# Weights' sums, key products and the gate-to-key transform change engines in the first stage of a hybrid encoder block

## The chip, the core and the metric

The kernel runs on one core of a Trainium2 chip. Its time is the device time of one execution in microseconds (us); of several executions the median is taken. TensorE (PE, with its weight load PEld) does the matmuls, VectorE (DVE), ScalarE (ACT) and GpSimd (POOL) the elementwise work, and SyncE (SP) issues most DMAs. Each engine works through its own instructions in order.

## The reference

One encoder block on 1024 tokens of width 1024, all float32. What matters here is one combined projection and what follows from it:

```
h = layer_norm(x)
p = h @ W_in        # 11776 columns: q/k/v of 3 head groups, HGRN q, f_fwd, f_bwd, i, g, 2 merge gates
a = dilated_attention(q, k, v)                       # 4 pairs of heads, three dilations
f = lb + (1 - lb) * sigmoid(f_pre);  k = 1 - f       # per direction; the gate gives the key
q_dec, k_inv = q * exp(cumsum(log f)), k * exp(-cumsum(log f))   # in chunks of 64 tokens
o = intra-chunk scores + state recurrence, forward and backward, 8 heads of 128
m = sigmoid(g_a) * (a @ W_a) + sigmoid(g_r) * (r @ W_r)
h = layer_norm(alpha * h + m @ W_o);  h = layer_norm(alpha * h + SwiGLU(h))
```

## The kernel before

The large products are done as Strassen-Winograd products of halves: seven products instead of eight for each 2x2 of blocks. Every operand is split into a high part (rounded to the fast float32 format) and the rest, and each product is three matmuls a 128-row block (`mm3`, L301 hi*hi, L302 hi weight * lo activation, L303 lo weight * hi activation).

The **first stage** (`phase1`, to about 1160 us of the span) makes the combined projection. `stream` runs over 23 sets of four 128-column tiles; in a set two groups `g` of two tiles each go through the products in the order 1, 2, 6, 5, 7, 3, 4. A product is 12 matmuls of 512 columns. Its weights are one of the four loaded blocks a11, a12, a21, a22 (128 partitions x 512, named `wa` in the profile) or one of the sums s1 = a21 + a22 (`ws`, L574), s3 = a11 - a21 (the **third sum**, L575, written over a21), s2 = s1 - a11 (L576, written over a11, so it comes after L575 has read a11) and s4 = a12 - s2 (L579). s2 is wanted by product 6, s3 only by product 7. For each product ScalarE casts the weights to `w_hi` (L585) and VectorE subtracts to `w_lo` (L590); four buffers of each exist, and the two are recorded three products ahead. Results leave PSUM by `keep` (ACT, L606) and by adds on VectorE (L475, L486, L507, L513).

Beside the stream runs the **side work**, a unit at a time: HGRN of a head, and the attention of a pair of heads. It fills the engines between the stream's instructions. `hgrn_dir` is run for each head and direction, 16 times. ScalarE makes four gate arrays from the loaded tanh (`t0` or `t1`, 128x1024; L1272, names fa, fb, qd, finv). Then the same tile is turned in place from gate to key, t3 = gna*t3 + ga (L1286). VectorE scans fa and fb into decays (L1291), t3's near half is multiplied by the decays R of fb (L1300), VectorE scans G (in qd), t3's far half is multiplied by G (L1303), VectorE scans finv, and two products with q (L1306, L1307) end it. Tiny copies of decays (`dec`, `both`, L1311 to L1314), memory sets and some small scalar work are GpSimd's. The key tile is then transposed on PE (L1322).

The order of each engine's instructions is set by a scheduler that models the engines at build time: the stream's casts, sums and evacuations have a priority 1000 instructions ahead, ScalarE's side work is kept behind the stream's latest (`behind`), and the first 14 products (`opening`) keep the order in which they are written.

Of the kernel before, what the change touches and what calls it, by code (L numbers as in the profile page):

```python
# [13 lines left out]
AF = mybir.ActivationFunctionType  # L14
OP = mybir.AluOpType
# [66 lines left out]
class Group:  # L82
# [25 lines left out]
    def product(self, n, bank, first):  # L108
        o = self.o
        if n not in self.made:  # L110
            self.prep(n)
        hi, lo = self.made.pop(n)
        xhi, xlo = o.xb[o.PRODUCTS[n][1]]
        if first:
            self.banks[bank] = o.ps_pj() if (bank == 2) != self.swap else o.ps_sd()
        ps = self.banks[bank]
        for k in range(4):
            o.mm3(ps, hi[:, k, :], lo[:, k, :], xhi[:, k, :], xlo[:, k, :], first and k == 0, k == 3,
                  skip_group_check=True)
        return ps  # L120
# [29 lines left out]
class Block:  # L150
# [405 lines left out]
    def stream(self, tiles):  # L556

        nc, tc = self.nc, self.tc
        self.cols = [c for c, _ in tiles]
        seq = [(n, g, p) for n in range(len(tiles) // 4) for p in self.ORDER for g in range(2)]  # L560
        after = {6: "a11", 7: "a21", 3: "a12", 4: "a22"}
        A = [{}, {}]
        state = [[{}, {}], [{}, {}]]
        ready = {}

        def sums(i, third=nc.gpsimd):
            if i >= len(seq):
                return
            n, g, p = seq[i]
            a = A[g]  # L570
            with tc.high_priority(offset=self.evac_ahead):
                if p == 6:
                    a["s1"] = self.blk.tile([128, 4, 128], F32, name="ws1", tag=f"s1{g}", bufs=1)
                    nc.vector.tensor_add(a["s1"], a["a21"], a["a22"])  # L574
                    third.tensor_sub(a["a21"], a["a11"], a["a21"])  # L575
                    nc.vector.tensor_sub(a["a11"], a["s1"], a["a11"])  # L576
                    a["s3"], a["s2"] = a["a21"], a["a11"]
                elif p == 3:
                    nc.vector.tensor_sub(a["a12"], a["a12"], a["s2"])  # L579
                    a["s4"] = a["a12"]  # L580

        def cast(i):
            n, g, p = seq[i]
            ready[i] = self.granules()
            nc.scalar.copy(ready[i][0], A[g][self.PRODUCTS[p][0]])  # L585

        def rest(i, e):
            n, g, p = seq[i]
            hi, lo = ready[i]
            e.tensor_sub(lo, A[g][self.PRODUCTS[p][0]], hi.bitcast(F32))  # L590
            if p in after and 4 * n + 4 < len(tiles):
                A[g][after[p]] = self.block(n + 1, g, after[p])

        def prep(i):
            if i >= len(seq):
                return
            with tc.high_priority(offset=self.evac_ahead):
                cast(i)
                rest(i, nc.vector)

        def bank(n, g, b):
            return self.ps_pj(2 * g + (n + b) % 2)

        def keep(ps, tag):
            t = self.ws.tile([128, HALF], F32, name="wkeep", tag=tag, bufs=1)
            nc.scalar.copy(t, ps)  # L606
            return t

        def product(i, h=None):
            n, g, p = seq[i]  # L610
            s = state[n % 2][g]
            if p in (1, 2) and h != 1:
                s[p] = bank(n, g, p)
            ps = s[1 if p in (1, 6, 7, 4) else 2]
            hi, lo = ready[i]
            if h != 0:
                del ready[i]
            c = slice(0, HALF) if h is None else slice(256 * h, 256 * h + 256)
            xhi, xlo = self.xb[self.PRODUCTS[p][1]]
            for k in range(4):  # L620
                self.mm3(ps[:, c], hi[:, k, :], lo[:, k, :], xhi[:, k, c], xlo[:, k, c],
                         p in (1, 2, 5) and k == 0 and h != 1, k == 3,
                         skip_group_check=True)

        def evacuate(i, *later):
            n, g, p = seq[i]
            s = state[n % 2][g]
            ps = s[1 if p in (1, 6, 7, 4) else 2]
            pair = [f for _, f in tiles[4 * n + 2 * g:4 * n + 2 * g + 2]]
            with tc.high_priority(offset=self.evac_ahead):  # L630
                if p in (1, 6):
                    s["u"] = keep(ps, f"k1{g}")
                elif p == 5:
                    s["m5"] = keep(ps, f"k5{g}")
                elif p == 2:
                    pair[0](0, ps, s["u"], *later)
                elif p == 7:
                    pair[1](1, ps, s["m5"])
                elif p == 3:
                    pair[0](1, ps, s["u"])  # L640
                else:
                    pair[1](0, ps, None)

        self.ahead_of = {}
        first = 2 * len(self.ORDER)
        with self.pool("p0") as pool:
            self.lasts = {}
            with self.in_order():
                self.opening(pool, A, {(g, p): i for i, (_, g, p) in enumerate(seq[:first])}, first, cast, rest, sums,
                             product, evacuate)  # L650
        yield 4
        sums(first + 4)
        for i, (n, g, p) in enumerate(seq):
            if i < first:
                continue
            with self.noted():
                sums(i + 5)
                prep(i + 3)
            if i < first + 2:
                continue  # L660
            product(i)
            evacuate(i)
            yield 4 * n + 2 * g + 2 if p == 4 else 0

    def opening(self, pool, A, at, first, cast, rest, sums, product, evacuate):

        nc, R = self.nc, self.rows_in(pool)
        dve, gps = nc.vector, nc.gpsimd
# [99 lines left out]
        R.sum("t1", 5)  # L768
        R.hi("t1", 5)
        R.copy(5, 1, "act")  # L770
        sums(at[0, 6], dve)
        R.turn(7, 0, 1)
        R.lo("t1", 5)
        cast(at[0, 6])
# [6 lines left out]
        R.sum("t1", 6)  # L781
        R.hi("t1", 6)
        product(at[0, 6], 0)
        sums(at[1, 6], dve)
        cast(at[1, 6])
        evacuate(at[0, 2], later)
        cast(at[0, 5])
# [464 lines left out]
    def hgrn_dir(self, h, d, st):  # L1252

        nc = self.nc
        ga, gb, gna = (z[:, d, h:h + 1] for z in (self.ga, self.gb, self.gna))
        t3 = st[f"t{d}"].rearrange("p (c i) -> p c i", i=128)
# [3 lines left out]
        far = slice(64, 128) if fwd else slice(0, 64)  # L1260
        near = slice(0, 64) if fwd else slice(64, 128)
# [3 lines left out]
        G = qd[:, 0:4, :].rearrange("p a (b i) -> p (a b) i", i=64)  # L1265
        H = self.half("finv").rearrange("p (c i) -> p c i", i=64)
        ends = self.half("ends").rearrange("p (c i) -> p c i", i=64)
        R = B[:, :, 1:65]

        def gates(f, one, to, of):  # L1270
            nc.gpsimd.memset(f[:, :, one:one + 1], 0.0)
            nc.scalar.activation(f[:, :, to], t3[:, :, of], AF.Identity, bias=gb, scale=ga)  # L1272
# [8 lines left out]
        else:  # L1281
# [1 line left out]
            gates(B, 0, slice(1, 66), slice(63, 128))  # L1283
            gates(G, 0, hi, slice(0, 63))
            gates(H, 63, lo, slice(64, 127))
        nc.gpsimd.tensor_scalar(t3, t3, gna, ga, op0=OP.mult, op1=OP.add)  # L1286

        def scan(f, at, rev):
            f = f.rearrange("p c i -> p (c i)")
            f = f[:, ::-1] if rev else f  # L1290
            nc.vector.tensor_tensor_scan(f, f, at, 0.0, op0=OP.mult, op1=OP.add)  # L1291

        def inverse(f, of, rev):

            nc.vector.reciprocal(ends[:, :, 0], of[:, ::-1] if rev else of)
            scan(f, ends.rearrange("p c i -> p (c i)"), rev)

        scan(A, self.d1[64], not fwd)
        scan(B, self.d1[66], fwd)
        nc.gpsimd.tensor_mul(t3[:, :, near], t3[:, :, near], R)  # L1300
        yield
        inverse(G, A[:, :, 63 if fwd else 0], fwd)
        nc.gpsimd.tensor_mul(t3[:, :, far], t3[:, :, far], G)  # L1303
        yield
        inverse(H, R[:, :, 0 if fwd else 63], not fwd)
        nc.vector.scalar_tensor_tensor(qd[:, :, far], q3[:, :, far], CQ, A, op0=OP.mult, op1=OP.mult)  # L1306
# [912 lines left out]
```

## Time and profile before

| | us |
|---|---|
| median of 3 runs | 2072.26 (2071.73 to 2073.45) |
| the profiled execution's own time | 2073.43 |
| its span | 2071.7 |
| busy: PE / DVE / ACT / POOL | 2013.5 / 1407.2 / 975.6 / 792.0 |

Busy time is summed over the whole span, which has stages with different limits; the first stage is about 56% of it. A matmul's span overlaps the next one's, so that 222 matmuls of 512 columns fill 50 us (0.226 us from start to start) though each is shown with about 0.39 us. In views by line, "mean ns" is that of one instruction; in views of a single line, three numbers are minimum, median and maximum. Waits of PE name the instruction that came last.

### The profile page before, as it was taken

The page shows a single profiled execution, that of the slowest core. Times are in us where ns is not written, and L with a number is a line of the kernel's source. Part 1 is how long each engine was busy: PE and PEld are TensorE (multiplying, and loading weights), DVE is VectorE, ACT ScalarE, POOL GpSimd, SP SyncE. Part 2 cuts the span into 40 slices and gives each one's busy share as a digit, 9 for nine tenths or more (in the row PEclk, how much of TensorE's full clock was granted, in tenths as well). Part 3 has the DMA queues.
Part 4 walks back from the last instruction along what each step waited for, and adds up shares of the span by engine and source line. Part 5 has one row for each costly group of instructions (what it writes and reads, how often), then busy time and mean ns, then how long its engine had stood idle before and what let it go on. Part 6 is the DMA issues. An engine that isn't in the chain of part 4 may idle for free.

```text
span 2071.7 us, 31393 instructions
## 1 busy us (share of the span) xinstructions
PE 2013.5 (97%) x11037; PEld 1672.6 (81%) x11037; DVE 1407.2 (68%) x2361; ACT 975.6 (47%) x2039; POOL 792.0 (38%) x694
## 2 busy tenths in 40 slices
PE   5999999999999999999999999999899999999998
PEld 5788888788888888888888788886788888888876
DVE  7778666776477855877556623457777776777864
ACT  7555456554564536655464421244444444444330
POOL 1134310343013330332100263243667767755563
PEclk9999999999999999999999999999999999999999
DMA  5433533445334352444436763335445444458684
GB/s 208 156 122 117 184 114 117 133 131 160 113 123 133 123 166 97 132 149 141 143 96 219 249 228 112 101 119 167 141 143 179 141 169 158 161 169 315 199 266 165
DMA packets 296448, 324.21 MB, mean 156 GB/s; under 512 B 15905, under 2 KB 212834, under 8 KB 296290
## 3 DMA queue, kind: packets, MB, share of 16 engines
q1 hardware_dynamic: 290272, 302.05, 45.2%
q10 hardware_dynamic: 6018, 20.16, 2.4%
q8 instruction: 87, 1.43, 0.3%
q14 instruction: 71, 0.58, 0.1%
HBM read 211.78 MB, written 110.36 MB: 156 GB/s over the span
## 4 chain that ended last, share of the span: by engine, by line
PE 77%; DVE 8%; DMA 5%; issue 4%; ACT 3%; POOL 2%; DVEq 0%; SPq 0%; ACTq 0%; POOLq 0%
PE pj L301 17%; PE pj L303 17%; PE pj L302 16%; PE sd L301 6%; PE sd L303 6%; PE sd L302 6%; PE sd L1391 2%; DVE w_lo L590 2%; DMA wa<-in_w_in_dram 2%; PE sd L1338 1%; POOL w_lo L280 1%; DMA ghi<-gs3h 1%; PE sd L1206 1%; ACT pf L1011 1%; PE sd L1131 1%
## 5 line engine op out<-in xcount | busy, mean ns | idle before, releaser
L590 DVE TENSOR_TENSOR w_lo<-wa,w_hi 128x512 fp32r<-128x512 f32 x273 | 213.8, 787 | 100.3 <-ACT w_hi L585 97.7
L585 ACT CAST w_hi<-wa 128x512 fp32r<-128x512 f32 x276 | 169.7, 618 | 215.4 <-PE pj L302 167.9
L280 POOL TENSOR_TENSOR w_lo<-f_raw,w_hi 128x512 fp32r<-128x512 f32 x110 | 176.0, 1611 | 107.1 <-ACT w_hi L276 45.7
L575 POOL TENSOR_TENSOR wa<-wa,wa 128x512 f32<-128x512 f32 x44 | 67.3, 1531 | 245.0 <-DVE ws L574 156.3
L301 PE MATMUL pj<-xt1hi,w_hi 128*128 128x512 f32 (+1 forms) x276 | 107.3, 389 | 0.0
L301 PE MATMUL pj<-xb22hi,w_hi 128*128 128x512 f32 x268 | 105.6, 394 | 1.6 <-ACT wkeep L606 1.6
L303 PE MATMUL pj<-xt1hi,w_lo 128*128 128x512 f32 (+1 forms) x276 | 106.3, 385 | 0.4 <-POOL w_lo L280 0.4
L302 PE MATMUL pj<-xt1lo,w_hi 128*128 128x512 f32 (+1 forms) x276 | 106.3, 385 | 0.0
L276 ACT CAST w_hi<-f_raw 128x512 fp32r<-128x512 f32 x110 | 67.9, 619 | 80.1 <-DVE f_raw L100 31.7
L302 PE MATMUL pj<-xb22lo,w_hi 128*128 128x512 f32 x268 | 104.8, 391 | 0.0
L303 PE MATMUL pj<-xb22hi,w_lo 128*128 128x512 f32 x268 | 104.7, 391 | 0.0
L280 POOL TENSOR_TENSOR w_lo<-Wb,w_hi 128x512 fp32r<-128x512 f32 x47 | 64.8, 1380 | 58.1 <-ACT w_hi L276 55.2
L606 ACT COPY wkeep<-pj 128x512 f32<-128x512 f32 x138 | 80.1, 581 | 8.6 <-DVE evh L513 3.9
L301 PE MATMUL pj<-xt2hi,w_hi 128*128 128x512 f32 (+1 forms) x196 | 77.9, 397 | 5.1 <-ACT w_hi L585 3.1
L301 PE MATMUL pj<-xb11hi,w_hi 128*128 128x512 f32 (+1 forms) x196 | 76.9, 392 | 3.3 <-ACT w_hi L585 2.5
L303 PE MATMUL pj<-xt2hi,w_lo 128*128 128x512 f32 (+1 forms) x196 | 76.6, 391 | 2.9 <-DVE w_lo L590 2.0
L303 PE MATMUL pj<-xb21hi,w_lo 128*128 128x512 f32 (+1 forms) x196 | 75.9, 387 | 3.4 <-DVE w_lo L590 3.4
L280 POOL TENSOR_TENSOR w_lo<-wsum,w_hi 128x512 fp32r<-128x512 f32 x44 | 66.9, 1520 | 30.2 <-ACT w_hi L276 26.3
L303 PE MATMUL pj<-xb11hi,w_lo 128*128 128x512 f32 (+1 forms) x196 | 76.5, 390 | 1.1 <-POOL w_lo L590 0.6
L302 PE MATMUL pj<-xt2lo,w_hi 128*128 128x512 f32 (+1 forms) x196 | 76.5, 390 | 0.7 <-DVE xt2lo L432 0.7
L301 PE MATMUL pj<-xb21hi,w_hi 128*128 128x512 f32 (+1 forms) x196 | 76.9, 392 | 0.1
L301 PE MATMUL pj<-xt3hi,w_hi 128*128 128x512 f32 x188 | 75.2, 400 | 1.5 <-ACT w_hi L276 1.5
(435 smaller groups left out, 6380.6 us busy)
## 6 DMA issues: line engine op xcount, KB each, us to landing
wa<-in_w_in_dram SPq DMA_DIRECT2D x184, 256.0 KB, 3.1
f_raw<-in_w_ffn_in_dram SPq DMA_DIRECT2D x44, 512.0 KB, 4.3
Wb<-in_w_ffn_out_dram SPq DMA_DIRECT2D x40, 256.0 KB, 5.3
tg<-evh SPq DMA_DIRECT2D x32, 256.0 KB, 2.1
tg<-tg SPq DMA_DIRECT2D x16, 512.0 KB, 4.3
y<-ahs SPq DMA_DIRECT2D x16, 512.0 KB, 4.1
ah<-xt SPq DMA_DIRECT2D x8, 512.0 KB, 6.5
rec<-hg ACTq DMA_DIRECT2D x8, 512.0 KB, 5.3
```

The source lines that it names most:

```text
L276: nc.scalar.copy(hi, src)
L280: e.tensor_sub(lo, src, hi.bitcast(F32))
L301: nc.tensor.matmul(ps, whi, xhi, start=first, stop=False, **kw)
L302: nc.tensor.matmul(ps, whi, xlo, start=False, stop=False, **kw)
L303: nc.tensor.matmul(ps, wlo, xhi, start=False, stop=last, **kw)
L575: third.tensor_sub(a["a21"], a["a11"], a["a21"])
L585: nc.scalar.copy(ready[i][0], A[g][self.PRODUCTS[p][0]])
L590: e.tensor_sub(lo, A[g][self.PRODUCTS[p][0]], hi.bitcast(F32))
L606: nc.scalar.copy(t, ps)
L1011: nc.scalar.activation(v, v, AF.Exp, bias=N12[:, hd, c:c + 1], scale=QSCALE, accum_out=l[:, hd, c:c + 1])
L1131: nc.tensor.matmul(ps[:, tt % 2, :], q[pb, 128 * tt - 64:128 * tt + 64], k[pb, 128 * (tt - 1):128 * (tt + 1)], start=True, stop=True)
L1391: nc.tensor.matmul(po[:, jj, :], l, r, start=(n == 0), stop=(n == len(terms) - 1))
```

## The change

Three things move, all in the first stage. The third sum L575 (128x512) of the stream's sets goes from GpSimd to VectorE: 44 of them; the two of the opening are there already. In `hgrn_dir` the transform L1286 (128x1024, in place) goes from GpSimd to ScalarE as one activation with a scale and a bias a partition (16), and the two products L1300 and L1303 (8 chunks of 64 on 128 partitions, in place) go from GpSimd to VectorE (32). The arithmetic stays as it is. GpSimd keeps the small scalar work, copies of decays and memory sets.

```
-        def sums(i, third=nc.gpsimd):
+        def sums(i):
...
                     nc.vector.tensor_add(a["s1"], a["a21"], a["a22"])
-                    third.tensor_sub(a["a21"], a["a11"], a["a21"])
+                    nc.vector.tensor_sub(a["a21"], a["a11"], a["a21"])
                     nc.vector.tensor_sub(a["a11"], a["s1"], a["a11"])
...
-        sums(at[0, 6], dve)
+        sums(at[0, 6])
...
-        sums(at[1, 6], dve)
+        sums(at[1, 6])
...
-        nc.gpsimd.tensor_scalar(t3, t3, gna, ga, op0=OP.mult, op1=OP.add)
+        nc.scalar.activation(t3, t3, AF.Identity, bias=ga, scale=gna)
...
         scan(B, self.d1[66], fwd)
-        nc.gpsimd.tensor_mul(t3[:, :, near], t3[:, :, near], R)
+        nc.vector.tensor_mul(t3[:, :, near], t3[:, :, near], R)
         yield
         inverse(G, A[:, :, 63 if fwd else 0], fwd)
-        nc.gpsimd.tensor_mul(t3[:, :, far], t3[:, :, far], G)
+        nc.vector.tensor_mul(t3[:, :, far], t3[:, :, far], G)
```

The scheduler orders all engines anew; the places are mostly near the moved instructions. Two of them matter below.

**VectorE, third head, from the `w_lo` of block 3718 to the `w_lo` of block 3871** (a12 of group 0, product 2). Before:

```order
L590 TENSOR_TENSOR w_lo_4063<-wa11_3718,w_hi_4062 128x512
L1291 SCALAR_TENSOR_TENSOR fa_3989<-fa_3989,d164_1153 128x512
L1291 SCALAR_TENSOR_TENSOR fb_4081<-fb_4081,d166_1156 128x528
L1306 SCALAR_TENSOR_TENSOR qd_3991<-q_3940,fa_3989 128x8x64
L1307 SCALAR_TENSOR_TENSOR qd_3991<-q_3940,finv_3992 128x8x64
L1295 RECIPROCAL ends_4084<-fa_3989 128x8
L576 TENSOR_TENSOR wa11_3718<-ws1_4124,wa11_3718 128x512
L513 SCALAR_TENSOR_TENSOR evh_4048<-evh_4048,wkeep_3844 128x512
L590 TENSOR_TENSOR w_lo_4103<-wa12_3871,w_hi_4102 128x512
```

With the change:

```order
L590 TENSOR_TENSOR w_lo_4063<-wa11_3718,w_hi_4062 128x512
L1306 SCALAR_TENSOR_TENSOR qd_3991<-q_3940,fa_3989 128x8x64
L1291 SCALAR_TENSOR_TENSOR fa_3989<-fa_3989,d164_1153 128x512
L576 TENSOR_TENSOR wa11_3651<-ws1_4098,wa11_3651 128x512
L1291 SCALAR_TENSOR_TENSOR fb_4081<-fb_4081,d166_1156 128x528
L575 TENSOR_TENSOR wa21_3851<-wa11_3718,wa21_3851 128x512
L1307 SCALAR_TENSOR_TENSOR qd_3991<-q_3940,finv_3992 128x8x64
L590 TENSOR_TENSOR w_lo_4103<-wa12_3871,w_hi_4102 128x512
```

Between the two L590 one L575 has come in; the reciprocal, the L513 and the L576 of group 1 have gone behind, and the L576 of group 0, which stood ahead, is in between.

**VectorE, fifth head, from the forward scan of finv to the `w_lo` of a22 (6117)**, group 0, product 4. Before:

```order
L1291 SCALAR_TENSOR_TENSOR finv_6535<-finv_6535,ends_6536 128x512
L590 TENSOR_TENSOR w_lo_6604<-wa12_6096,w_hi_6603 128x512
L1291 SCALAR_TENSOR_TENSOR fa_6532<-fa_6532,d164_1153 128x512
L1291 SCALAR_TENSOR_TENSOR fb_6626<-fb_6626,d166_1156 128x528
L1295 RECIPROCAL ends_6629<-fa_6532 128x8
L507 TENSOR_TENSOR wkeep_6569<-wkeep_6569,pj_6331 128x512
L1291 SCALAR_TENSOR_TENSOR qd_6627<-qd_6627,ends_6629 128x512
L1306 SCALAR_TENSOR_TENSOR qd_6534<-q_6487,fa_6532 128x8x64
L1307 SCALAR_TENSOR_TENSOR qd_6534<-q_6487,finv_6535 128x8x64
L1295 RECIPROCAL ends_6629<-fb_6626 128x8
L590 TENSOR_TENSOR w_lo_6644<-wa22_6117,w_hi_6643 128x512
```

With the change:

```order
L1291 SCALAR_TENSOR_TENSOR finv_6535<-finv_6535,ends_6536 128x512
L1300 TENSOR_TENSOR t0_6485<-t0_6485,fb_6533 128x8x64
L1303 TENSOR_TENSOR t0_6485<-t0_6485,qd_6534 128x8x64
L590 TENSOR_TENSOR w_lo_6575<-wa12_6036,w_hi_6574 128x512
L1306 SCALAR_TENSOR_TENSOR qd_6534<-q_6487,fa_6532 128x8x64
L1307 SCALAR_TENSOR_TENSOR qd_6534<-q_6487,finv_6535 128x8x64
L590 TENSOR_TENSOR w_lo_6604<-wa12_6096,w_hi_6603 128x512
L1291 SCALAR_TENSOR_TENSOR fa_6532<-fa_6532,d164_1153 128x512
L1291 SCALAR_TENSOR_TENSOR fb_6626<-fb_6626,d166_1156 128x528
L507 TENSOR_TENSOR wkeep_6569<-wkeep_6569,pj_6331 128x512
L1295 RECIPROCAL ends_6629<-fa_6532 128x8
L590 TENSOR_TENSOR w_lo_6644<-wa22_6117,w_hi_6643 128x512
```

The forward products L1300 and L1303 have come in, the `w_lo` of 6036 has gone behind them, and the scan of the backward G (qd) and the second reciprocal have gone behind the last `w_lo`.

**ScalarE, third head, backward direction**, from the last gate on, with the change:

```order
L1272 ACTIVATE finv_4083<-t1_3942,gb_1146,ga_1145 128x8x63
L585 CAST w_hi_4102<-wa12_3871 128x512
L510 ACTIVATE evh_4048<-wkeep_3844 128x512
L489 ACTIVATE evh_4078<-pj_3632 128x512
L1286 ACTIVATE t1_3942<-t1_3942,ga_1145,gna_1147 128x1024
L585 CAST w_hi_4128<-wa12_3948 128x512
```

The L1286 stands between two of the stream's casts; before, it was not on this engine, and L510 stood ahead of the first cast.

## The prediction

> **What bounds the kernel now.** I read the page first:
>
> ```profile
> span 2071.7 us, 31393 instructions
> PE 2013.5 (97%) x11037; PEld 1672.6 (81%) x11037; DVE 1407.2 (68%) x2361; ACT 975.6 (47%) x2039; POOL 792.0 (38%) x694
> ```
>
> PE sets the time, and only what PE waits for in the first stage can be won: the change touches no matmul. So next come PE's waits from 100 to 1155 us (waiter, releaser, us in total, times, longest):
>
> ```profile
> PE pj L303 <- DVE w_lo L590: 6.8, 3, 3.4
> PE sd L1368 <- DVE hR L1352: 1.4, 1, 1.4
> ```
>
> All end with VectorE, most of them with a late `w_lo`. Where they are and what they cost is shown by the engines' busy time in stretches of 2.5 us (PE, PEld, DVE, ACT, POOL, then granted clock, DMA share, GB/s):
>
> ```profile
> 377.50:380.00 2.50, 2.24 (x19) 1.80 (x17) 2.50 (x5) 0.00 (x0) 2.50 (x2) 1.00 0.00 0
> 380.00:382.50 2.50, 0.00 (x0) 0.00 (x0) 2.50 (x3) 1.51 (x3) 2.50 (x4) 1.00 0.06 22
> 382.50:385.00 2.50, 1.87 (x5) 1.48 (x6) 2.50 (x4) 1.62 (x4) 1.34 (x3) 0.67 0.50 188
> 385.00:387.50 2.50, 2.50 (x9) 1.99 (x8) 2.50 (x4) 0.43 (x1) 0.94 (x1) 0.64 0.00 0
> ...
> 627.50:630.00 2.50, 1.88 (x15) 1.45 (x13) 2.50 (x2) 0.00 (x0) 2.42 (x3) 1.00 0.00 0
> 630.00:632.50 2.50, 0.26 (x1) 0.26 (x2) 2.50 (x4) 0.00 (x0) 1.63 (x1) 1.00 0.00 0
> 632.50:635.00 2.50, 2.50 (x7) 1.95 (x7) 2.50 (x4) 1.59 (x3) 0.00 (x0) 0.51 0.59 165
> 635.00:637.50 2.50, 2.50 (x10) 1.99 (x10) 2.50 (x6) 0.64 (x3) 0.00 (x0) 0.81 0.91 320
> ...
> 1157.50:1160.00 2.50, 1.20 (x6) 0.66 (x4) 2.50 (x4) 2.50 (x6) 0.00 (x0) 1.00 0.21 62
> ```
>
> Two stalls stand out, in the third and the fifth head. PE is idle 0.26 + 2.50 + 0.63 = 3.39 us in the first and 0.62 + 2.24 = 2.86 us in the second, and after each the granted clock is down: (0.33 + 0.36) x 2.5 = 1.7 us and (0.49 + 0.19) x 2.5 = 1.7 us of full-speed work lost. Together 9.65 us. In both VectorE is busy without a break and GpSimd beside it. A third place, at the stage's end, loses 1.3 us.
>
> Now VectorE's timeline ahead of the first stall (start, us, instruction), and GpSimd's:
>
> ```profile
> 366.00 1.25 DVE L1291 TENSOR_TENSOR_SCAN fb<-fb,d 128x528 f32<-128x528 f32 x1
> ...
> 373.68 1.14 DVE L590 TENSOR_TENSOR w_lo<-wa,w_hi 128x512 fp32r<-128x512 f32 x1
> 374.74 1.22 DVE L1291 TENSOR_TENSOR_SCAN fa<-fa,d 128x512 f32<-128x512 f32 x1
> 375.88 2.29 DVE L1291 TENSOR_TENSOR_SCAN fb<-fb,d 128x528 f32<-128x528 f32 x1
> 378.09 0.66 DVE L1306 SCALAR_TENSOR_TENSOR qd<-q,fa 128x512 f32<-128x512 f32 x1
> 378.67 0.68 DVE L1307 SCALAR_TENSOR_TENSOR qd<-q,finv 128x512 f32<-128x512 f32 x1
> 379.27 0.19 DVE L1295 RECIPROCAL ends<-fa 128x8 f32<-128x8 f32 x1
> 379.39 1.50 DVE L576 TENSOR_TENSOR wa<-ws,wa 128x512 f32<-128x512 f32 x1
> 380.81 0.68 DVE L513 SCALAR_TENSOR_TENSOR evh<-evh,wkeep 128x512 f32<-128x512 f32 x1
> 381.41 1.67 DVE L590 TENSOR_TENSOR w_lo<-wa,w_hi 128x512 fp32r<-128x512 f32 x1
> ```
>
> ```profile
> 374.85 2.21 POOL L575 TENSOR_TENSOR wa<-wa,wa 128x512 f32<-128x512 f32 x1
> 377.00 1.16 POOL L1311 COPY dec<-fa 128x8 f32<-128x8 f32 x1
> 380.90 1.62 POOL L1300 TENSOR_TENSOR t<-t,fb 128x512 f32<-128x512 f32 x1
> ```
>
> The last `w_lo` is the one PE waits for; it ends at 383.08. The same kind of instruction takes 0.68 or 1.7 us, and a scan 1.2 or 2.3 us, here while GpSimd works. All of the stage, by line (minimum, median, maximum in ns):
>
> ```profile
> L590 DVE TENSOR_TENSOR w_lo<-wa,w_hi x273: 620/686/1797, 28.4 to 1177.8; 128x512 fp32r<-128x512 f32 x137
> L486 DVE TENSOR_TENSOR evh<-wkeep,pj x48: 660/680/690, 48.3 to 1182.6; 128x512 f32<-128x512 f32 x48
> ```
>
> L590 has two inputs in SBUF and reaches 1797 ns; L486, of the same size with one input in PSUM, never goes over 690. So the excess looks like GpSimd and VectorE shutting each other out of SBUF, not like a slow instruction. The Trainium skill says so (SBUF — State Buffer, "SBUF: two separate sides"): a VectorE instruction with two SBUF inputs and a GpSimd one that reads SBUF take one shared port pair in turn, each for its whole length. By that rule a collision costs up to a whole GpSimd instruction and the term below is nearly all of its upper bound; the two rows agree, though they do not show which GpSimd instructions shut VectorE out.
>
> **What the change removes.** From GpSimd 44 third sums, 16 transforms and 32 products go. Grouped by line and shape, 60 to 1155 us (count | busy, mean ns | idle before):
>
> ```profile
> L575 POOL TENSOR_TENSOR wa<-wa,wa 128x512 f32<-128x512 f32 x43 | 66.1, 1537 | 245.0 <-DVE ws L574 156.3 <-DMA wa<-in_w_in_dram 17.0 <-ACT pf L1011 14.2
> L1303 POOL TENSOR_TENSOR t<-t,qd 128x512 f32<-128x512 f32 x16 | 30.8, 1925 | 3.0 <-DVE qd L1291 2.9
> L1286 POOL TENSOR_SCALAR t<-t,gna,ga 128x1024 f32<-128x1024 f32 x16 | 30.1, 1884 | 2.6 <-POOL fb L1271 2.6
> L1300 POOL TENSOR_TENSOR t<-t,fb 128x512 f32<-128x512 f32 x16 | 28.3, 1767 | 0.7 <-DVE fb L1291 0.2
> L590 DVE TENSOR_TENSOR w_lo<-wa,w_hi 128x512 fp32r<-128x512 f32 x261 | 205.5, 791 | 98.3 <-ACT w_hi L585 95.7 <-PE sd L974 2.0 <-PE sd L1028 0.3
> L1291 DVE TENSOR_TENSOR_SCAN finv<-finv,ends 128x512 f32<-128x512 f32 x16 | 26.9, 1680 | 0.5
> ```
>
> GpSimd loses 66.1 + 30.8 + 30.1 + 28.3 = 155 us, all its large work of the stage except the attention bias and one small add. If the excess goes with it, VectorE gets back (791 - 686) x 261 = 27.4 us in L590, and with 1.22 us as the undisturbed scan (the row at 374.74) (1.68 - 1.22) x 16 = 7.4 in one of the four scans: 35 us in these two groups, more with the rest. The bounds of that term are nothing and all of it.
>
> **What it adds.** On VectorE 44 + 32 = 76 instructions of 128x512 from SBUF. Their nearest rows are L576 for the sum and L1306 for the products (the same chunks of 64), both undisturbed about 0.68 us, 0.60 from start to start (378.09, 378.67, 379.27): 76 x 0.60 = 46 us. So VectorE's total hardly moves, -35 + 46 = +11 us at most. What counts is the place. In a head's stretch GpSimd's work is dense, and each L1300 or L1303 removed costs VectorE 0.6 us where a collision costs 0.8 to 1.1.
>
> Ahead of the first stall: from the scan at 366.00 to the `w_lo` at 373.68 VectorE took 7.68 us; in the new order it holds two scans (1.25, 1.22), seven instructions of 0.66 to 0.69 and a reciprocal, about 7.4, less 0.08 of overlap for each, 6.6 us. From there the order shown gives 0.69 + 0.66 + 1.22 + 0.69 + 1.25 + 0.69 + 0.68 = 5.9, less 0.6 of overlap, 5.3 us instead of 7.73. The late `w_lo` then ends at 366.0 + 6.6 + 5.3 + 0.7 = 378.6, and PE, which was idle for the last 0.26 us before 380, wanted it at 379.7: the 3.39 us go, with 1 us to spare. The fifth head's stretch runs from one scan of fb to the `w_lo` that PE waits for:
>
> ```profile
> 617.38 1.26 DVE L1291 TENSOR_TENSOR_SCAN fb<-fb,d 128x528 f32<-128x528 f32 x1 [2.61 <-ACT fb L1272]
> ...
> 630.55 1.63 DVE L590 TENSOR_TENSOR w_lo<-wa,w_hi 128x512 fp32r<-128x512 f32 x1
> ```
>
> It ends at 632.2. In the new order that scan, a reciprocal and the eleven rows shown stand ahead of it: four scans 4.9, two reciprocals 0.4, seven of 0.66 to 0.69 together 4.7, so 10.0 less 1.0 of overlap; it ends at 617.4 + 9.0 + 0.7 = 627.1, against a need at 629.4. But the two `w_lo` that follow come with little or no margin, since the products of the backward direction and the next s1, whose blocks must have landed, now stand ahead of them. At the stage's end L576 waits for an L575 of 3.96 us on GpSimd:
>
> ```profile
> L575 POOL TENSOR_TENSOR wa<-wa,wa x44: 1274/1416/3961, 85.3 to 1155.3; 128x512 f32<-128x512 f32 x44
> ```
>
> On VectorE it takes 0.7, so I count 1 of the 1.3 us there as won.
>
> On ScalarE 16 activations of 128x1024 with scale and bias a partition:
>
> ```profile
> L324 ACT ACTIVATE xt<-xt,mv x8: 1237/1242/1252, 8.3 to 38.5; 128x1024 f32<-128x1024 f32 x8
> L585 ACT CAST w_hi<-wa 128x512 fp32r<-128x512 f32 x261 | 160.5, 618 | 203.9 <-PE pj L302 163.2 <-issue 18.5 <-DVE wa L576 9.1
> ```
>
> The first is the same function, shape and operands: 1.24 us, 16 x 1.24 = 20 us. The casts stand idle 203.9 us, 163 of them until PE frees a buffer, so a cast that comes 1.24 us later is covered three products ahead, by about 12 x 0.226 = 2.7 us each. Without that cover it would cost 1.24 us a time. L1300 must now wait for ScalarE, not for GpSimd; in the orders shown L1286 follows the last gates closely, while VectorE has scans ahead of L1300. If it did not, the next `w_lo` would be queued behind it. No DMA is issued elsewhere, and SP's order changes at a few neighbours only.
>
> **The sum.** Two stalls with their clock -9.65, the stage's end -1.0, and for new small stalls behind the two places and in other heads +3.0 (two of the 1.4 us that the waits show as a small one, rounded up): -7.65 us. The profiled execution took 2073.43 us, 1.2 above the median; its stalls are taken as those of a median run, so 2072.26 - 7.65 = 2064.6, say **2064.5 us**.
>
> **The rivals.** (1) *The stalls only move* (0.14). For it: margins of about 1 us, and VectorE no less busy in total. Against it: the two places have 2 to 4 us less ahead of the late `w_lo`. Half of the idle time and one loss of clock would stay: -9.65 / 2 - 1 + 3 = -2.8, or 2069.5; with a little more, 2071.
>
> (2) *ScalarE is late* (0.10): L1286 stands ahead of casts and of L1300. Against it the casts' 163 us of waiting for PE. If half of the 16 find no cover, 8 x 1.24 = 10 us eat the gain: 2074; it decides where PE's waits name L585 in the heads.
>
> (3) *VectorE becomes the bound*, the other side (0.08). In a head it is nearly full:
>
> ```profile
> 850.00:900.00 50.00, 50.00 (x300) 42.52 (x297) 43.04 (x67) 27.95 (x60) 18.52 (x17) 1.00 0.48 157
> ```
>
> If the excess is not GpSimd's large work, or the tiny copies left there (L1311, 1.16 us) keep causing it, each head gets four products and two sums, 6 x 0.60 = 3.6 us, ahead of a `w_lo`: the two stalls grow by 3.6 and two more heads begin to stall at 3.6 + 1.7 of clock: 7.2 + 10.6 = +18, or 2090; half of it, 2081. It decides once the mean of L590 stays over some 0.75 us. The Trainium skill warns that way (Perfetto Trace Analysis, "Optimizing Scalar/DVE Operations"): work should leave a saturated VectorE, though the same section doubts that GpSimd helps.
>
> **How the numbers follow.** The forecast has 0.68; its own range is 2058 (no new stalls, and some of the small ones gone) to 2068.5. With (1) and the near end of (2) the range is 2057.5 to 2072. A measurement of this kernel tells about 0.2%, 4.1 us. Faster: 0.66 of the forecast, 0.03 of (1) and 0.01 of (2), 0.70. The same: 0.02, 0.11 and 0.06, 0.19. Slower: 0.03 of (2) and 0.08 of (3), 0.11.
>
> **What would show it.** Right: L590 with mean near 0.70 us and hardly one over 1 us; the scans all near 1.2; no stretch in the third and fifth heads with the clock under 1.00; PE waits on L590 of 2 to 4 us in the stage; GpSimd's busy time down by about 155 us or more. Wrong: a PE wait on L585 or behind L1300, or an L590 still at 1.7 us beside a small GpSimd copy.

## The result, and the profile after

The changed kernel takes 2057.11 us (median of 4 runs, 2054.89 to 2059.24) beside 2072.86 us of the kernel before (4 runs in the same set). The ratio is 0.9929, with a 95% interval of 0.9917 to 0.9941: 14.7 us faster, about twice the 7.65 that the sum gave.

The page of the changed kernel, which shows the fastest of its runs, 2054.89 us:

```profile
span 2053.1 us, 31298 instructions
PE 2009.0 (98%) x11037; PEld 1671.5 (81%) x11037; DVE 1401.7 (68%) x2437; ACT 995.8 (49%) x2055; POOL 641.3 (31%) x602
```

The span is 18.6 us shorter (4 us of that beyond the 14.7, as the page before shows a run of 2073.43 us, a little slower than its median, and this page the fastest run). VectorE is as busy as before (1401.7 and 1407.2), and only GpSimd has much less to do. The first stage in one stretch (PE, PEld, VectorE, ScalarE, GpSimd, then granted clock, DMA share, GB/s), before:

```profile
100.00:1150.00 1050.00, 1039.08 (x6676) 870.78 (x6675) 734.07 (x1492) 568.25 (x1326) 270.01 (x317) 1.00 0.43 138
```

and after:

```profile
100.00:1150.00 1050.00, 1049.55 (x6740) 881.59 (x6739) 743.19 (x1588) 596.95 (x1358) 127.53 (x229) 1.00 0.44 142
```

PE was idle for 10.92 us of this stretch and is idle for 0.45 now. The view of PE's waits from 100 to 1155 us, which showed five kinds before, has no row left. The places of the two stalls, in stretches of 2.5 us:

```profile
377.50:380.00 2.50, 2.50 (x18) 2.17 (x17) 2.50 (x4) 2.31 (x5) 1.99 (x2) 1.00 0.43 159
380.00:382.50 2.50, 2.40 (x16) 1.79 (x15) 2.50 (x6) 0.40 (x1) 2.42 (x2) 1.00 0.14 51
382.50:385.00 2.50, 2.50 (x12) 2.06 (x11) 2.50 (x5) 1.26 (x4) 0.24 (x1) 1.00 0.28 105
...
627.50:630.00 2.50, 2.50 (x15) 2.15 (x14) 2.50 (x5) 0.75 (x2) 0.00 (x0) 1.00 0.98 347
630.00:632.50 2.50, 2.50 (x22) 2.41 (x21) 2.50 (x5) 2.38 (x6) 0.00 (x0) 1.00 0.31 115
```

VectorE is still busy without a break, PE works through, and the clock stays at 1.00. The subtractions and scans (the first row from the groups by line, 60 to 1155 us; the others give minimum, median and maximum over the whole run):

```profile
L590 DVE TENSOR_TENSOR w_lo<-wa,w_hi 128x512 fp32r<-128x512 f32 x266 | 185.4, 699 | 102.7 <-ACT w_hi L585 99.4 <-PE sd L974 2.0 <-PE sd L1338 0.9
...
L1291 DVE TENSOR_TENSOR_SCAN finv<-finv,ends x16: 1205/1220/1247, 126.6 to 924.4; 128x512 f32<-128x512 f32 x16
L1286 ACT ACTIVATE t<-t,ga,gna x16: 1230/1248/1257, 124.5 to 921.3; 128x1024 f32<-128x1024 f32 x16
L575 DVE TENSOR_TENSOR wa<-wa,wa x46: 653/684/693, 40.3 to 1138.4; 128x512 f32<-128x512 f32 x46
```

The mean of L590 fell from 791 to 699 ns; the scan of finv, which had a mean of 1680, now never goes over 1247. VectorE's timeline in the third head, up to the `w_lo` that came late before, and GpSimd's beside it:

```profile
368.90 1.25 DVE L1291 TENSOR_TENSOR_SCAN fb<-fb,d 128x528 f32<-128x528 f32 x1
...
376.65 1.22 DVE L1291 TENSOR_TENSOR_SCAN fa<-fa,d 128x512 f32<-128x512 f32 x1
377.79 0.67 DVE L576 TENSOR_TENSOR wa<-ws,wa 128x512 f32<-128x512 f32 x1
378.37 1.25 DVE L1291 TENSOR_TENSOR_SCAN fb<-fb,d 128x528 f32<-128x528 f32 x1
379.54 0.67 DVE L575 TENSOR_TENSOR wa<-wa,wa 128x512 f32<-128x512 f32 x1
380.12 0.68 DVE L1307 SCALAR_TENSOR_TENSOR qd<-q,finv 128x512 f32<-128x512 f32 x1
380.72 0.68 DVE L590 TENSOR_TENSOR w_lo<-wa,w_hi 128x512 fp32r<-128x512 f32 x1
```

```profile
377.93 1.68 POOL L1311 COPY dec<-fa 128x8 f32<-128x8 f32 x1 [7.24 <-DVE fa L1291]
379.68 2.38 POOL L1312 COPY dec<-fb 128x8 f32<-128x8 f32 x1
```

Every instruction of VectorE has its undisturbed length. The small copies beside them take 1.68 and 2.38 us, where the shortest of their kind takes 0.19: here GpSimd waits for VectorE, and no wait for these copies shows in the profile.

### The profile page after: what moved, and what is told of

It reads as the page before. It is cut to its first block, busy times and chain, and to the rows that moved or that the text cites. A ratio compares the mean times of both kernels' runs of the same rounds, so it can differ in the third digit from the quotient of the medians.

```text
span 2053.1 us, 31298 instructions
## 1 busy us (share of the span) xinstructions
PE 2009.0 (98%) x11037; PEld 1671.5 (81%) x11037; DVE 1401.7 (68%) x2437; ACT 995.8 (49%) x2055; POOL 641.3 (31%) x602
## 4 chain that ended last, share of the span: by engine, by line
PE 74%; issue 2%; DVE 1%; POOL 1%; DMA 1%; ACT 1%; DVEq 0%; POOLq 0%; ACTq 0%
PE pj L301 16%; PE pj L303 16%; PE pj L302 16%; PE sd L301 6%; PE sd L302 6%; PE sd L303 6%; PE sd L1391 1%; POOL w_lo L280 1%; PE sd L1338 1%; PE sd L1131 1%; PE sd L907 1%; PE sd L1206 1%; PE sd L1322 0%; PE sd L1186 0%; ACT pf L1011 0%
## 5 line engine op out<-in xcount | busy, mean ns | idle before, releaser
L585 ACT CAST w_hi<-wa 128x512 fp32r<-128x512 f32 x276 | 169.5, 617 | 218.5 <-PE pj L302 174.3
L590 DVE TENSOR_TENSOR w_lo<-wa,w_hi 128x512 fp32r<-128x512 f32 x273 | 190.2, 699 | 104.8 <-ACT w_hi L585 101.4
L1373 POOL TENSOR_TENSOR ham<-amx,amy 64x256 f32<-64x256 f32 x16 | 11.6, 728 | 249.4 <-DVE amy L1371 249.4
L280 POOL TENSOR_TENSOR w_lo<-w_raw,w_hi 128x512 fp32r<-128x512 f32 x32 | 44.0, 1379 | 117.0 <-ACT w_hi L276 117.0
L302 PE MATMUL pj<-xb11lo,w_hi 128*128 128x512 f32 (+1 forms) x196 | 76.0, 388 | 0.0
```

The lines of the kernel that those rows point to most:

```text
L280: e.tensor_sub(lo, src, hi.bitcast(F32))
L302: nc.tensor.matmul(ps, whi, xlo, start=False, stop=False, **kw)
```

## The experiments

Two theories were set against each other. **C** (collisions): VectorE loses time to GpSimd instructions that read SBUF, and the change wins what that cost. **O** (order): the scheduler has put the instructions in another order, and the order wins, wherever the work is done. They can be told apart because PE's order hangs on one edit: with the third sums on VectorE and either or both of the other moves undone it stays that of the changed kernel (but for one place where the transform alone is undone), and with the third sums on GpSimd it is word for word that of the kernel before, whatever else moves.

### Each of the three moves alone, and GpSimd's work without its reads

Third sums alone on VectorE (products and transform as before):

```
-                    third.tensor_sub(a["a21"], a["a11"], a["a21"])
+                    nc.vector.tensor_sub(a["a21"], a["a11"], a["a21"])
```

> Only the 44 third sums go to VectorE; the transform and the products stay on GpSimd. PE's order is that of the changed kernel, row for row. Theory C (GpSimd's large reading instructions and VectorE's with two SBUF inputs shut each other out, and this alone makes w_lo late): the scans still reach 2.2 us and the two stalls in the third and fifth heads stay in part, L590's mean falls from 791 to about 745 ns, time 2064 to 2069 us. Theory O (the new order and the shorter chain from s1 to s2 make the gain): all of it is here, 2056 to 2059 us.

Products alone on VectorE:

```
-        nc.gpsimd.tensor_mul(t3[:, :, near], t3[:, :, near], R)
+        nc.vector.tensor_mul(t3[:, :, near], t3[:, :, near], R)
...
-        nc.gpsimd.tensor_mul(t3[:, :, far], t3[:, :, far], G)
+        nc.vector.tensor_mul(t3[:, :, far], t3[:, :, far], G)
```

> Only the 32 products L1300 and L1303 go to VectorE. PE's order is that of the kernel before, row for row. Theory C: the collisions in the heads fall by about half, L575's in the attention parts stay, time 2062 to 2068 us. Theory O: PE's order and the sums' chain are as before, 2070 to 2075 us.

Transform alone on ScalarE:

```
-        nc.gpsimd.tensor_scalar(t3, t3, gna, ga, op0=OP.mult, op1=OP.add)
+        nc.scalar.activation(t3, t3, AF.Identity, bias=ga, scale=gna)
```

> Only the 16 transforms go to ScalarE. PE's order is that of the kernel before, row for row. The transform has one input, and few slow VectorE instructions lay beside it alone. Theory C: a small gain at most, 2067 to 2073 us. Theory O: 2071 to 2074 us. If ScalarE's added 20 us delay casts (rival 2 of the prediction): over 2074 us, with PE waits on L585.

The kernel before with GpSimd as busy at the same places, but with memory sets and an 8-column copy in place of the sums, the transform and the products (so third sums and keys are not computed in it):

```
-                    third.tensor_sub(a["a21"], a["a11"], a["a21"])
+                    [third.memset(a["a21"][:, 0:z, :], 0.0) if z else third.tensor_copy(a["a21"][:, 0, 0:8], a["a11"][:, 0, 0:8]) for z in (4, 4, 2, 0)]
...
-        nc.gpsimd.tensor_scalar(t3, t3, gna, ga, op0=OP.mult, op1=OP.add)
+        [nc.gpsimd.memset(t3[:, 0:z, :], 0.0) for z in (8, 4)]
...
-        nc.gpsimd.tensor_mul(t3[:, :, near], t3[:, :, near], R)
+        [nc.gpsimd.memset(t3[:, :, near], 0.0) if z else nc.gpsimd.tensor_copy(t3[:, :, near][:, :, 0:1], R[:, :, 0:1]) for z in (3, 2, 1, 0)]
```

and the far half with G in the same way.

> The kernel before, with GpSimd's third sums, transforms and products replaced by memory sets of the same tile and of about the same length, each followed by a copy of 8 columns from the second input, so that every wait stays; the sums and keys are not computed. GpSimd is as busy as before but hardly reads SBUF. Theory C: L590's mean falls to about 700 ns and the stalls go, 2056 to 2062 us. Theory O, or a theory that GpSimd's length and waits make VectorE late: 2069 to 2075 us.

Measured, beside 2072.68 us of the kernel before: third sums alone 2072.21 us, ratio 0.9996 (0.9987 to 1.0005); products alone 2063.28, 0.9953 (0.9941 to 0.9966); transform alone 2064.38, 0.9956 (0.9944 to 0.9969); memory sets 2055.01, 0.9917 (0.9904 to 0.9931).

O falls twice. The third sums alone bring the changed kernel's PE order and gain nothing; the memory sets gain all of it with orders near the kernel before's (about 1 in 300 of PE's instructions and 1 in 20 of VectorE's stand elsewhere). For C the last is the cleanest case. Its stage:

```profile
100.00:1150.00 1050.00, 1048.71 (x6740) 880.86 (x6739) 700.26 (x1513) 577.80 (x1343) 265.65 (x557) 1.00 0.44 142
...
L590 DVE TENSOR_TENSOR w_lo<-wa,w_hi 128x512 fp32r<-128x512 f32 x266 | 184.8, 698 | 117.0 <-ACT w_hi L585 114.7 <-PE sd L974 2.0
```

GpSimd is busy for 265.65 us there, as before (270.01), but does not read the large tiles any more, and L590 is at 698 ns. So it is not GpSimd's busy time that costs, but what it reads.

But C missed two sizes. It expected the third sums to be worth something and the transform little. With the third sums alone moved, the third head is as bad as ever (stretches, then VectorE, then GpSimd):

```profile
380.00:382.50 2.50, 2.03 (x17) 1.59 (x15) 2.50 (x4) 0.00 (x0) 1.89 (x2) 1.00 0.00 0
382.50:385.00 2.50, 0.03 (x1) 0.04 (x1) 2.50 (x5) 1.19 (x3) 1.79 (x3) 0.84 0.00 0
385.00:387.50 2.50, 2.50 (x6) 2.02 (x7) 2.50 (x5) 1.94 (x4) 0.10 (x1) 0.50 0.28 105
```

```profile
377.12 1.53 DVE L575 TENSOR_TENSOR wa<-wa,wa 128x512 f32<-128x512 f32 x1
...
382.03 1.67 DVE L576 TENSOR_TENSOR wa<-ws,wa 128x512 f32<-128x512 f32 x1
383.63 0.68 DVE L513 SCALAR_TENSOR_TENSOR evh<-evh,wkeep 128x512 f32<-128x512 f32 x1
384.23 0.68 DVE L590 TENSOR_TENSOR w_lo<-wa,w_hi 128x512 fp32r<-128x512 f32 x1
```

```profile
375.50 2.61 POOL L1286 TENSOR_SCALAR t<-t,gna,ga 128x1024 f32<-128x1024 f32 x1
...
381.68 1.47 POOL L1300 TENSOR_TENSOR t<-t,fb 128x512 f32<-128x512 f32 x1 [0.16 <-DVE fb L1291]
```

The transform stretches L575 to 1.53 us and the product stretches L576 to 1.67; each would be 0.68. The late `w_lo` itself is not disturbed at all: it is late because of what stands ahead of it.

In the fifth head of this run PE does not wait for a `w_lo` but for the transposed key, which ScalarE copies out of PSUM:

```profile
PE sd L1338 <- ACT hkT L1323: 3.1, 1, 3.1
```

VectorE is behind this one too: ahead of the copy in ScalarE's order stands an evacuation (L489) that has waited 2.96 us for VectorE's L486. With the transform alone moved, and with the products brought back (below), PE waits there in the same way for 2.04 and 1.84 us. So a late `w_lo` is one way from a stretched VectorE to PE, and a late evacuation that holds up ScalarE is another.

### Which GpSimd work counts: the changed kernel with one move undone

Theory C was made sharper, in the words of the expectations: only a collision ahead of a late `w_lo` costs time (the late evacuation above belongs with it). Third sums back on GpSimd:

```
-                    nc.vector.tensor_sub(a["a21"], a["a11"], a["a21"])
+                    (nc.gpsimd if i >= 14 else nc.vector).tensor_sub(a["a21"], a["a11"], a["a21"])
```

> The changed kernel with one of its three moves undone: the 44 third sums are GpSimd's again, transform and key products stay where the change has put them. TensorE's order is then word for word that of the kernel before, not that of the changed kernel. Theory C (only GpSimd's reads ahead of a late w_lo cost time): the heads' long GpSimd work is gone, so neither the third nor the fifth head stalls for over 1 us and no clock under 1.00 stands there; the collisions with L575 stay, some 15 us in sum, and cost a few small stalls: 2056 to 2062. Theory O (the new order is what wins, and the third sum sets it): the old order of TensorE brings stalls of 2 us or more back in the heads: 2064 to 2070.

Products back on GpSimd:

```
-        nc.vector.tensor_mul(t3[:, :, near], t3[:, :, near], R)
+        nc.gpsimd.tensor_mul(t3[:, :, near], t3[:, :, near], R)
...
-        nc.vector.tensor_mul(t3[:, :, far], t3[:, :, far], G)
+        nc.gpsimd.tensor_mul(t3[:, :, far], t3[:, :, far], G)
```

> The changed kernel with the 32 key products on GpSimd again, third sums and transform where the change has put them. TensorE's order is word for word that of the changed kernel. Theory C: L1300 and L1303 lie ahead of the late w_lo of a head and stretch scans and subtractions there; with L575 and L1286 gone their collisions begin earlier, with more margin, so less than in the kernel before: 2060 to 2067, with PE idle 3 to 8 us from 100 to 1155 us. Theory O (the order of the changed kernel is what wins): as the changed kernel, 2055 to 2059, and PE idle under 1 us there.

The transform back on GpSimd, and, to see whether ScalarE matters for it, on VectorE:

```
-        nc.scalar.activation(t3, t3, AF.Identity, bias=ga, scale=gna)
+        nc.gpsimd.tensor_scalar(t3, t3, gna, ga, op0=OP.mult, op1=OP.add)
```

> The changed kernel with the 16 transforms back on GpSimd. Theory C: a one-input instruction of 1.2 us beside VectorE's busiest stretches; a few collisions of up to 1 us in the heads, 2056 to 2063 us. Theory O: as the changed kernel, 2055 to 2059 us.

```
-        nc.scalar.activation(t3, t3, AF.Identity, bias=ga, scale=gna)
+        nc.vector.tensor_scalar(t3, t3, gna, ga, op0=OP.mult, op1=OP.add)
```

> The changed kernel with the 16 transforms on VectorE. No trace has this instruction; a 128x256 scaling takes 0.34 us there (L1172), so 0.6 to 1.2 us each, 10 to 20 us more on VectorE's fullest stretches and 20 less on ScalarE. If VectorE still has slack: 2055 to 2060 us. If the margin of about 1 us ahead of the w_lo is real: a stall comes back in one or two heads, 2060 to 2066 us.

All eight combinations of the three moves, and the transform on VectorE. Idle and clock are PE's losses from 100 to 1150 us, summed over stretches of 2.5 us of each profiled run (idle: 2.5 less PE's busy time; clock: 2.5 times what the granted clock lacks to 1). Excess is what VectorE's instructions take over the tenth percentile of their own kind (line and operands), where that is over 0.15 us, from 60 to 1160 us. L475 is not counted: it takes 0.66 or some 1.05 us in every run alike, with the change or without.

| moved off GpSimd | median, us | ratio (95%) | idle | clock | excess |
|---|---|---|---|---|---|
| nothing (before) | 2072.15 to 2072.86 | 1 | 10.9 | 3.4 | 54.0 |
| third sums | 2072.21 | 0.9996 (0.9987 to 1.0005) | 10.6 | 5.2 | 31.1 |
| transform | 2064.38 | 0.9956 (0.9944 to 0.9969) | 5.8 | 1.7 | 48.4 |
| products | 2063.28 | 0.9953 (0.9941 to 0.9966) | 5.1 | 0 | 30.1 |
| third sums, transform | 2062.61 | 0.9959 (0.9946 to 0.9973) | 5.5 | 0 | 29.1 |
| third sums, products | 2061.03 | 0.9941 (0.9926 to 0.9956) | 4.4 | 0 | 10.3 |
| transform, products | 2058.02 | 0.9928 (0.9916 to 0.9941) | 1.8 | 0 | 21.7 |
| all three (the change) | 2057.11 | 0.9929 (0.9917 to 0.9941) | 0.45 | 0 | 4.5 |
| all three, transform on VectorE | 2059.91 | 0.9937 (0.9924 to 0.9951) | 2.6 | 0 | 3.9 |

Three readings. First, take PE's loss off the median, and with it what three kernels lose at the stage's end, from 1150 to 1165 us (1.96 us before, 0.9 with the products alone moved, 0.3 with the transform alone): 2055.9 to 2057.3 us are left in all nine rows. To within 1.4 us, which is less than the spread of one kernel's runs, the stage's stalls and the clock that they cost are the whole difference. Second, the third sums gain nothing that stands clear of the noise in any of the four pairs: 0.9996 alone; 0.9956 and 0.9959 without and with them beside the transform; 0.9953 and 0.9941 beside the products, with intervals that overlap; 0.9928 and 0.9929 beside both, where the two traces differ by 1.4 us of idle. Alone they do end the loss at the stage's end, but the clock then costs 1.7 us more in the third head. In the kernel where only they stayed on GpSimd the collisions are there, and PE does not feel them:

```profile
100.00:1150.00 1050.00, 1048.19 (x6736) 879.46 (x6735) 733.90 (x1543) 593.26 (x1354) 180.61 (x271) 1.00 0.43 142
...
L590 DVE TENSOR_TENSOR w_lo<-wa,w_hi 128x512 fp32r<-128x512 f32 x266 | 195.6, 738 | 103.7 <-ACT w_hi L585 101.0 <-PE sd L974 2.0 <-PE sd L1028 0.3
...
PE sd L1193 <- DVE p L932: 0.9, 1, 0.9
PE pj L303 <- DVE w_lo L590: 0.7, 2, 0.4
```

The excess is 21.7 us, about three quarters of it beside L575, and PE's waits are 1.6 us together. Where only transform and third sums were moved, 29.1 us of excess, most of it beside L1300 and L1303, go with 5.5 us of idle PE. So neither the sum of the collisions nor the mean of L590 tells the cost; the place does. Third, the gains don't add: transform and products are worth some 9 us each alone and 15 together. Either of them cuts the long stalls (10.9 us of idle fall to 5.8 or 5.1) and half or all of the lost clock; both together leave 1.8 us. This refutes O once more: the products brought back keep the changed kernel's PE order and are slower (2062.61), the third sums brought back have PE's old order and are as fast (2058.02).

Whether the transform's own engine matters is not settled by the times: on ScalarE 0.9929, on VectorE 0.9937, on GpSimd 0.9941, with intervals that overlap.

### Reading alone, added to the changed kernel

Two kernels add work on GpSimd to the changed kernel, at the places where the moved work had stood; it goes into a scratch tile that nobody reads, and the kernel's own results are computed as in the changed one. In the first the work reads SBUF:

```
+ [nc.gpsimd.tensor_add(self.junk.rearrange("p (k c) -> p k c", k=2), a["s1"][:, z:z + 2, :], a["s1"][:, z:z + 2, :]) for z in (0, 2) if i >= 14]
...
+ [nc.gpsimd.tensor_scalar(self.junk, st["q"][:, 256 * z:256 * z + 256], gna, ga, op0=OP.mult, op1=OP.add) for z in range(4)]
...
+ [nc.gpsimd.tensor_mul(self.junk.rearrange("p (c i) -> p c i", i=64), R[:, z:z + 4, :], R[:, z:z + 4, :]) for z in (0, 4)]
```

(and the same with A after the far product).

> The changed kernel, and beside it GpSimd works as before on a scratch tile nobody reads: behind each third sum two adds of 128x256 (both inputs s1), behind each transform four scalings of 128x256 of q, behind each product two products of 128x256. Nothing waits for them, and VectorE's order is the changed kernel's but for some 60 of 2439 instructions. Theory C: collisions come back, L590's mean over 760 ns and maxima of 1.3 us and more, stalls come back, 2064 to 2074 us. Theory O: nothing waits for it, 2056 to 2060 us.

In the second it is memory sets behind an 8-column copy of the same source:

```
+ [nc.gpsimd.memset(self.junk, 0.0) if z else nc.gpsimd.tensor_copy(self.junk[:, 0:8], a["s1"][:, 0, 0:8]) for z in range(6) if i >= 14]
...
+ [nc.gpsimd.memset(self.junk, 0.0) if z else nc.gpsimd.tensor_copy(self.junk[:, 0:8], R[:, 0, 0:8]) for z in range(7)]
```

(and so with q and A).

> The same places, but GpSimd writes memory sets to the scratch tile (five or six of 128x256 behind a copy of 8 columns) and does not read. Theory C: no collisions beyond the tiny copies, L590's mean near 700 ns, 2055 to 2060 us. If writes of GpSimd shut VectorE out as reads do: like load_reads, over 2064 us. Theory O: 2056 to 2060 us.

Measured: with reads 2086.83 us, ratio 1.0068 (1.0052 to 1.0084), slower than the kernel before; with memory sets 2058.8, 0.9933 (0.9919 to 0.9946), as the changed kernel. With reads:

```profile
100.00:1150.00 1050.00, 1030.79 (x6614) 862.30 (x6614) 753.81 (x1547) 580.32 (x1329) 335.28 (x437) 0.99 0.41 133
...
L590 DVE TENSOR_TENSOR w_lo<-wa,w_hi 128x512 fp32r<-128x512 f32 x257 | 188.1, 734 | 92.9 <-ACT w_hi L585 90.0 <-PE sd L974 2.0 <-PE sd L1028 0.3
...
PE sd L1368 <- DVE hR L1352: 4.7, 3, 1.7
PE sd L1365 <- DVE hR L1352: 3.3, 2, 2.0
PE sd L1338 <- ACT hkT L1323: 2.9, 1, 2.9
```

With memory sets:

```profile
100.00:1150.00 1050.00, 1048.15 (x6730) 879.69 (x6729) 738.50 (x1582) 595.09 (x1356) 326.12 (x817) 1.00 0.43 140
...
L590 DVE TENSOR_TENSOR w_lo<-wa,w_hi 128x512 fp32r<-128x512 f32 x264 | 183.4, 697 | 101.0 <-ACT w_hi L585 97.2 <-PE sd L974 2.0 <-PE sd L1338 0.9
...
L575 POOL MEMSET junk<- 128x256 f32 x220 | 68.7, 312 | 12.7
```

GpSimd is busy for 335 and 326 us: nearly the same load, 28 us apart, with VectorE's order in both that of the changed kernel but for some 60 instructions. VectorE's excess, counted as in the table, is 44.4 us beside the reads and about 3 beside the memory sets. That is C's direction, but the size went past the expected 2064 to 2074: PE's loss is 26.0 us (19.2 idle, 6.8 of clock) with an excess less than the 54.0 of the kernel before, which loses 14.3. The reads also hold ws, q, fb and fa for longer than an 8-column copy does, and PE's waits name the HGRN state (hR) first, not `w_lo`. How much of the 26 us is collision and how much is a source tile that is held was not separated.

No run points to a version faster than the changed kernel: the stage has 0.45 us of idle PE left.

## Why the prediction was right in its direction and short in its size

**The mechanism was right.** The two edits that mattered won by ending collisions. The predicted signs are there: L590's mean at 699 ns ("near 0.70"), 7 of them over 1 us from 60 to 1155 us where there were 37, scans near 1.2, no clock under 1.00 in the two heads. VectorE's busy time in the stage rose by 9.1 us ("+11 at most"), the activation takes 1.248 (1.24), and no PE wait names L585. GpSimd's busy time fell by 150.7 us in the whole run, 142.5 in the stage, not 155: its small copies got longer, those of L1311 and L1312 from 19.4 to 28.0 us together up to 1160 us. Of the upper bound of 35 us for the excess in L590 and the scan of finv, (791 - 699) x 261 = 24.0 and 7.4 went, nearly all.

**The two long stalls, −9.65: right**, and by the working shown. From the scan to the end of the late `w_lo` the third head takes 381.40 − 368.90 = 12.5 us (12.6 predicted). The fifth, by these rows, takes 621.50 − 611.61 = 9.9 (9.7):

```profile
611.61 1.26 DVE L1291 TENSOR_TENSOR_SCAN fb<-fb,d 128x528 f32<-128x528 f32 x1 [3.06 <-ACT fb L1272]
...
620.85 0.65 DVE L590 TENSOR_TENSOR w_lo<-wa,w_hi 128x512 fp32r<-128x512 f32 x1
```

The margin in the third head was not 1 us, though: the head starts 2.9 us later in the span, behind a weight block, and PE comes 1.6 us later too; PE still waits 0.1 us there.

**What failed is the term "+3.0 for new small stalls", and what was not counted beside it.** No new stall came: the stage's idle is 0.45 us in all, and of the 2 to 4 us of waits on L590 that were to be left, none is. And the small stalls that were there (1.39 us at 475, 0.86 at 692, 1.65 around 1100, and others) were left in the sum as if they stayed; idle and clock of before are 14.33 us from 100 to 1150, so 14.33 − 9.65 = 4.68 us stood outside the two stalls, and all of it went. At the stage's end 1.96 us went, not 1.0: there the sum had only one of the places. So −9.65 − 4.68 − 1.96 + 0.45 = −15.8 from the traces, against 14.7 by the ratio and 15.75 by the medians. The mistake was to price the change at two places that had been looked at, and to let the margin there stand for the other heads. Every head has the same instructions; what freed VectorE in two freed it in all. The range had this case at its near end (2058, "no new stalls, and some of the small ones gone"); the measured median lies just below that, and 0.4 us below the 2057.5 with which the whole range was closed. That the time came out at the edge of the range and not well outside it is in part luck: 4.68 us had no term in the sum.

**One cause was credited with too much.** The third sums were the largest block removed (66.1 of the 155 us), the working of the third head gains from the scan that an L575 had stretched, and the stage's end was put down to an L575 of 3.96 us. At the stage's end that reading holds: with the third sums alone moved, PE works through it. But it was not the only way there, since with L575 left on GpSimd and the other two moved the end loses 0.4 us, and in the time the runs give the third sums nothing. What had to go were the transform or the products, best both.

**The rivals.** *The stalls only move* is what happens when the third sums alone move, so it was a real case, for another change. *ScalarE is late* did not show. *VectorE becomes the bound* did not show, and its condition about the small copies did not either: those left on GpSimd do not lengthen VectorE's instructions, they wait themselves. In this kernel 32 products moved off GpSimd onto a VectorE that is nearly full in the heads gain 9.7 us alone (ratio 0.9953), and VectorE's busy time from 100 to 1150 us stays what it was (734.07 and 735.74): the collisions that went paid for them. The Trainium skill (Perfetto Trace Analysis, "Optimizing Scalar/DVE Operations") doubts that moving work between the two helps; that doubt is right here for work that goes to GpSimd (2062.61 us with the products brought back, against 2057.11), and not the other way.

## What to carry to other kernels

Where one kind of VectorE instruction shows a wide spread of durations, look at what GpSimd reads at the same moment, and take that work to any engine that has room, even VectorE, if the instruction is shorter there than the collision. Don't price it by the sum of the excess: look for the deadline that the stretched instructions stand ahead of (an operand that PE waits for, or an evacuation that holds up another engine), and expect the second of two such edits to win only what the first has left. When a stall is explained by a pattern that repeats in every block of work, count all its small copies in the trace before adding a margin against them.

## What the runs showed of the hardware

**Only GpSimd's reads collide.** Of 326 to 335 us of GpSimd work, VectorE's instructions show an excess of 44.4 us when it reads and of about 3 us when it sets memory; the times are 28 us apart, though part of that may be the tiles that the reads hold. VectorE instructions with an input in PSUM (L486, L507) never take more than 0.694 us in any of the twelve traces. That is as the Trainium skill has it (SBUF — State Buffer, "SBUF: two separate sides": the shared ports are held for a whole instruction, and a VectorE instruction with two SBUF inputs meets only a GpSimd one that reads SBUF). The exclusion goes both ways, which the prediction had not used:

```profile
L1312 POOL COPY dec<-fb x16: 190/192/5456, 124.2 to 922.0; 128x8 f32<-128x8 f32 x16
```

In the changed kernel a copy of 8 columns with a median of 0.192 us once takes 5.456, beside a VectorE that does not pause.

**The clock is lost in pieces of 1.7 us, after single waits of about 2 us and more.** With the transform alone moved, PE waits once for 2.04 us (0.92 + 1.12 in two stretches), and a loss follows:

```profile
630.00:632.50 2.50, 1.58 (x7) 0.96 (x6) 2.50 (x5) 1.53 (x4) 0.89 (x1) 1.00 0.84 261
632.50:635.00 2.50, 1.38 (x12) 1.39 (x13) 2.50 (x5) 2.36 (x6) 1.98 (x1) 0.99 0.72 267
635.00:637.50 2.50, 2.50 (x13) 2.50 (x13) 2.50 (x4) 2.47 (x8) 1.66 (x1) 0.50 0.20 74
637.50:640.00 2.50, 2.50 (x10) 2.04 (x10) 2.50 (x5) 1.44 (x4) 0.00 (x0) 0.83 0.02 6
```

(0.01 + 0.50 + 0.17) x 2.5 = 1.7 us, as after each stall of the kernel before; with the third sums alone moved the third head loses (0.16 + 0.50 + 0.50 + 0.21) x 2.5 = 3.4, twice that. What counts is the length of one wait and not the idle time of a place: 0.64 + 1.44 us from 477.5 to 482.5 us with the third sums alone moved are two waits, the longer 1.72 us, and cost no clock; neither do 0.94 + 1.84 us in the fifth head with the products brought back, nor 1.24 + 1.72 us at 916 us with the added reads. From 60 to 1200 us the twelve traces have eight waits of 2.04 to 3.39 us, each with a loss behind it, and none of 1.84 us or less is followed by one, but for a wait of 1.72 us that stands inside the loss of the wait before it. Just above 2 us it is not certain: of eight waits of 2.05 to 2.07 us in the next stage seven have the loss and one has not. The Trainium skill (TensorE: Matmul & The Clock Gate, "What's actually happening") tells of a free-running window of about 3.4 us, at half clock after an idle one: half of it is 1.7 us, which agrees, and a free-running window would explain that waits of the same length sometimes cost and sometimes not; that is argued, no run here shows the window. By these traces a wait of 2 to 3 us, shorter than a window, is already enough.
